# Tail of a hybrid decoder block: the norm's multiply moves from GpSimd to VectorE, token tile 0's scaling to ScalarE, and the last pieces change order

## Chip, cores and metric

One core of a Trainium2 chip runs the kernel. The time is device microseconds of one execution, median of several. Engines: PE (TensorE) multiplies matrices, VectorE (DVE) and ScalarE (ACT) work element by element, GpSimd (POOL) likewise, SyncE (SP) issues the transfers.

## What is computed

A block of 256 tokens and width 2048 in float32. The last stage, which the change touches, takes the merged branches, multiplies by one more matrix, adds the residual with a gate and normalises each token's row:

```python
merged = jax.nn.sigmoid(g_a) * y_a + jax.nn.sigmoid(g_b) * y_b
x = x + gate[:, None, :] * (merged @ w_out[l])
...
def rms_norm(x, w):
    xf = x.astype(jnp.float32)
    y = xf * lax.rsqrt(jnp.mean(xf * xf, axis=-1, keepdims=True) + EPS)
    return (y * w.astype(jnp.float32)).astype(x.dtype)
...
return rms_norm(x, normf_w)
```

So each output row needs the sum of squares over all of its 2048 columns before any of it can be scaled and stored.

## The kernel before

The kernel streams its weights as units of 128 x 1024 in the order of a list, `UNITS`. Each float32 weight is split by ScalarE and VectorE into a high and a low part (L288, L294), and PE multiplies three times (high by high, low by high, high by low; L322 and L334). Instructions are issued to each engine's queue in the order in which the Python code writes them; an engine takes its queue in that order, and waits are inserted where one instruction overwrites or reads what another engine reads or writes.

The output projection is the last stage: 32 units, k = 0 to 15 by two halves of 1024 columns. There are two token tiles, t = 0 and 1, of 128 tokens each. For each token tile and half there is one PSUM tile of two banks (`cur[t, half]`, 2 x 512 columns). In units with k under 12 both token tiles are multiplied as the weights come; the weights of the last four k (`KEEP`) are kept in SBUF (keepH, keepL), and there token tile 0 is finished first (L888) and evicted in four chunks of 512 columns (L892).

Then comes the tail (L898 to L916): token tile 1's last four k, piece by piece in the order of `TAIL` (L45). A piece (lo, n) covers n columns from lo; lo under 1024 is half 0, lo from 1024 on half 1, and within a half 512 columns make a bank. So 0 is half 0, first bank; 512 and 768 are half 0, second bank; 1024 and 1280 are half 1, first bank; 1536 and 1792 are half 1, second bank. Each piece is 4 x 3 matmuls (L906), followed by its eviction, `out_evac`:

- L765, VectorE: r = PSUM times the gate;
- L766, VectorE: r = r + residual;
- L772, ScalarE: Square of r, summed over the columns into one number per token (a second instruction, the accumulator read, belongs to it); the squares themselves overwrite the residual, which is done with;
- L774, GpSimd: r = r times the norm's weights, in place. For tile 1's columns from 1536 on this is left to L804.

After the first piece `out_root(0)` adds up tile 0's sums (L791, VectorE) and takes the root (L792, ScalarE). Two calls of `out_finish(0, ...)`, after the third and the fourth piece, scale tile 0: a reciprocal (L799, VectorE), then for even chunks L806 on VectorE, for odd ones L808 on ScalarE, each with its store (L809, SyncE). `out_partial` (L783 to L786, VectorE) sums tile 1's numbers as far as they are there, `out_root(1)` (L794, ScalarE) and `out_finish(1, ...)` end the kernel with a reciprocal, four scalings and four stores.

Of the kernel before, what the change touches and what calls it, by code (L numbers as in the profile page):

```python
# [19 lines left out]
AF = mybir.ActivationFunctionType  # L20
ALU = mybir.AluOpType
PSUM = bass.MemoryType.PSUM

S, D, NH, DK, DV = 256, 2048, 8, 128, 256
# [17 lines left out]
KEEP = 4  # L42
WARM = (9, 16)

TAIL = ((0, 512), (1024, 512), (512, 256), (1536, 256), (768, 256), (1792, 256))  # L45


def units():
# [26 lines left out]
def alt(x):  # L75

    return x.rearrange("p (a n) -> p n a", a=2)
# [13 lines left out]
def body(ctx: ExitStack, tc: tile.TileContext, wu, wa, xT_d, x_d, cols_d, rows_d, out_d):  # L91
    nc = tc.nc
    act, dve, pool, pe, sync = nc.scalar, nc.vector, nc.gpsimd, nc.tensor, nc.sync
# [9 lines left out]
    def slot(tag, shape, name, dt=F32):  # L103
        return slots.tile(shape, dt, name=name, tag=tag)
# [83 lines left out]
    for i in range(2):  # L188
        cp = psum("g", f"c{i}")
        cps.append(cp)  # L190
        for b in range(2):
            lo = 1024 * i + 512 * b
# [132 lines left out]
    def stationary(a, k, t):  # L325

        return a[:, k, 128 * t:128 * t + 128] if a is hH or a is hL else a[:, k, t:S:2]
# [13 lines left out]
    def run_fillers(n):  # L341
        for _ in range(min(n, len(fillers) + len(later))):
            (fillers or later).popleft()()
# [388 lines left out]
    fin = {}  # L732
# [23 lines left out]
    def out_evac(t, lo, n, p):  # L756

        if "r" not in fin:
            fin["r"] = slot("s7", [128, 2, D], "r")
            fin["ss"] = slot("fss", [128, 2, 4], "fss")  # L760
            fin["ssl"] = slot("fssl", [128, 4], "fssl")
            fin["tot"] = slot("tot", [128, 2, 1], "tot")
        cs = slice(lo, lo + n)
        r, x = fin["r"][:, t, cs], ml["x"][:, t, cs]
        dve.tensor_tensor(r, p, fin["gate_b"][:, cs], op=ALU.mult)  # L765
        dve.tensor_tensor(r, r, x, op=ALU.add)  # L766
        if n == 512:
            ss = fin["ss"][:, t, lo // 512:lo // 512 + 1]
        else:
            i = TAIL.index((lo, n)) - len(TAIL) + 4  # L770
            ss = fin["ssl"][:, i:i + 1]
        act.activation(x, r, AF.Square, accum_out=ss)  # L772
        if not t or lo < 1536:
            pool.tensor_tensor(r, r, norm_row(lo, n), op=ALU.mult)  # L774

    def norm_row(lo, n):
        return fin["nf", lo // 1024][:, lo % 1024:lo % 1024 + n]

    def out_partial(step):

        ss, sl = fin["ss"][:, 1, :], fin["ssl"]
        if step == 0:
            dve.tensor_scalar(ss[:, 1:2], ss[:, 0:1], ss[:, 2:3], sl[:, 0:1], op0=ALU.add, op1=ALU.add)  # L783
        else:
            dve.tensor_scalar(ss[:, 1:2], ss[:, 1:2], sl[:, 1:2], sl[:, 2:3], op0=ALU.add, op1=ALU.add)
            dve.tensor_scalar(ss[:, 3:4], ss[:, 1:2], 1.0 / D, EPS, op0=ALU.mult, op1=ALU.add)  # L786

    def out_root(t):
        tot = fin["tot"][:, t, :]
        if t == 0:  # L790
            dve.tensor_reduce(tot, fin["ss"][:, t, :], axis=mybir.AxisListType.X, op=ALU.add)  # L791
            act.activation(tot, tot, AF.Sqrt, bias=eps_c, scale=1.0 / D)  # L792
        else:
            act.activation(tot, fin["ssl"][:, 3:4], AF.Sqrt, bias=fin["ss"][:, t, 3:4], scale=1.0 / D)  # L794

    def out_finish(t, chunks):
        tot = fin["tot"][:, t, :]
        if 0 in chunks:
            dve.reciprocal(tot, tot)  # L799
        for c in chunks:  # L800
            cs = slice(512 * c, 512 * c + 512)
            r = fin["r"][:, t, cs]
            if t and c == 3:
                dve.scalar_tensor_tensor(r, r, tot, norm_row(512 * c, 512), op0=ALU.mult, op1=ALU.mult)  # L804
            elif c % 2 == 0:
                dve.tensor_scalar(r, r, tot, None, op0=ALU.mult)  # L806
            else:
                act.activation(r, r, AF.Copy, scale=tot)  # L808
            sync.dma_start(out_d[128 * t:128 * t + 128, cs], r)  # L809
# [7 lines left out]
    for n, (kind, grp, k, half) in enumerate(UNITS):  # L817
# [28 lines left out]
        elif kind == "if":  # L846
# [4 lines left out]
            for b in range(8):  # L851
                kk = 8 * k + b
                c = slice(128 * b, 128 * b + 128)
# [28 lines left out]
        else:  # L882
# [6 lines left out]
            if kept:  # L889
                if k == 15:  # L890
                    for b in range(2):
                        out_evac(0, 1024 * half + 512 * b, 512, cur[0, half][:, b, :])  # L892
            else:
                mm_token(cur[1, half], w, 0, hb["mH"], hb["mL"], k, 1, k == 0, False)
                head.pop(n)
                rest.pop(n)
            run_fillers(len(fillers) if kept else 1)
    for lo, n in TAIL:  # L898
        half, c0 = divmod(lo, 1024)
        b, at_b = divmod(c0, 512)  # L900
        p = cur[1, half][:, b, at_b:at_b + n]
        for k in range(16 - KEEP, 16):
            u = NU - 2 * (16 - k) + half
            for a, w in ((hb["mH"], head[u]), (hb["mH"], rest[u]), (hb["mL"], head[u])):
                wb = alt(w[:, 512 * b:512 * b + 512])[:, at_b // 2:(at_b + n) // 2, :]
                pe.matmul(p, lhsT=stationary(a, k, 1), rhs=wb, start=False,  # L906
                          stop=k == 15 and w is head[u] and a is hb["mL"], skip_group_check=True)
        out_evac(1, lo, n, p)
        if (lo, n) == TAIL[0]:
            out_root(0)  # L910
        elif (lo, n) in TAIL[2:4]:
            out_finish(0, (0, 1) if (lo, n) == TAIL[2] else (2, 3))
        if (lo, n) in (TAIL[3], TAIL[5]):
            out_partial(TAIL.index((lo, n)) - 3)
    out_root(1)
    out_finish(1, (0, 2, 1, 3))  # L916


# [59 lines left out]
```

## Time and profile before

| | us |
|---|---|
| median of 3 runs | 1179.76 (1177.83 to 1180.12) |
| the profiled execution | 1177.47 |
| its span, first to last instruction | 1175.8 |
| PE busy | 1152.4 (98%) |
| VectorE busy | 809.7 (69%) |
| ScalarE busy | 572.7 (49%) |
| GpSimd busy | 16.6 (1%) |
| first eviction begins (L765) | 1152.81 |
| last matmul begins | 1166.97 |

The shares are means over stages with different limits; for a change in the tail only the last 24 us count. In rows of the timeline the first number is the start in us from the start of the span, the second the duration; a row with xN merges N instructions that follow each other; brackets give how long the engine was idle before the row and which instruction's end released it. A busy PE is not PE at its peak. PEclk is the clock granted to PE as a share of 2.4 GHz.

### The profile page before, as it was taken

To read this page: it belongs to the slowest core of one execution; us is meant where nothing else is said; L and a number is where in the kernel's file an instruction comes from. 1 tells how busy PE (TensorE), PEld (TensorE's weight loads), DVE (VectorE), ACT (ScalarE), POOL (GpSimd) and SP (SyncE) were. 2 spreads that over 40 slices of the span, in tenths; PEclk is the share of its full clock that TensorE was granted. 3 is DMA by queue.
4 is the path that set the end of the run, shared out by engine and by line. 5 is a ranking of instruction groups with operands and counts; after the bars stand their busy time and mean duration, and the time that the engine had idled before them with its cause. 6 is when DMAs were issued, how large, how long until landed. Compare 5 with 4: busy or idle time off the path is not lost.

```text
span 1175.8 us, 21120 instructions
## 1 busy us (share of the span) xinstructions
PE 1152.4 (98%) x8738; PEld 1103.6 (94%) x8738; DVE 809.7 (69%) x1000; ACT 572.7 (49%) x670; POOL 16.6 (1%) x26
## 2 busy tenths in 40 slices
PE   8999999999999999999999999999999999999996
PEld 7898889988888999999999999999999999999995
DVE  6889998876888966655587465565564555556466
ACT  6754344464353556444556643533533443444452
POOL 0000000000000000000000000000000000000003
PEclk9999999999999999999999999999999999999999
DMA  9999899888788855544457556566556555486652
GB/s 342 389 382 361 324 367 357 310 324 298 256 319 306 317 198 182 196 151 156 162 178 268 196 184 214 182 198 210 188 197 205 197 196 191 144 289 219 219 204 72
DMA packets 79905, 283.57 MB, mean 241 GB/s; under 512 B 10689, under 2 KB 10817, under 8 KB 79425
## 3 DMA queue, kind: packets, MB, share of 16 engines
q1 hardware_dynamic: 79810, 282.23, 67.6%
q8 instruction: 68, 1.11, 0.4%
q14 instruction: 27, 0.22, 0.1%
HBM read 280.09 MB, written 2.11 MB: 240 GB/s over the span
## 4 chain that ended last, share of the span: by engine, by line
PE 80%; DVE 4%; issue 1%; DMA 1%; ACT 0%; DVEq 0%; SPq 0%; ACTq 0%
PE gB L322 7%; PE u L322 7%; PE yB L322 7%; PE yA L322 7%; PE C L322 7%; PE zb L322 7%; PE B L322 7%; PE qk L322 7%; PE out L334 6%; PE z L334 5%; PE gA L322 5%; PE o L334 2%; DVE wl L294 1%; PE v L334 1%; PE num L573 1%
## 5 line engine op out<-in xcount | busy, mean ns | idle before, releaser
L294 DVE TENSOR_TENSOR wl<-raw,wh 128x1024 fp32r<-128x1024 f32 x408 | 495.7, 1222 | 301.5 <-ACT wh L288 299.2
L288 ACT ACTIVATE wh<-raw 128x1024 fp32r<-128x1024 f32 x409 | 431.4, 1059 | 471.3 <-PE yB L322 47.0
L247 DVE SCALAR_TENSOR_TENSOR ada<-ada,c_b 128x1024 f32<-128x1024 f32 x96 | 116.9, 1218 | 1.2 <-DMA ada<-wa 1.2
L322 PE MATMUL gB<-hH,wh 128*128 128x256 f32 x256 | 40.0, 279 | 0.7 <-ACT wh L288 0.7
L334 PE MATMUL o<-wh,hH 128*128 128x512 f32 x128 | 38.2, 380 | 2.0 <-DVE v_ext L383 1.6
L334 PE MATMUL v<-wh,hH 128*128 128x512 f32 x128 | 38.2, 380 | 1.5 <-DVE o L383 1.5
L322 PE MATMUL gB<-hH,wl 128*128 128x256 f32 x256 | 39.2, 276 | 0.1
L322 PE MATMUL B<-hH,wh 128*128 128x256 f32 x256 | 39.3, 276 | 0.0
L334 PE MATMUL v<-wl,hH 128*128 128x512 f32 x128 | 38.2, 380 | 1.1 <-DVE wl L294 1.1
L322 PE MATMUL u<-hH,wh 128*128 128x256 f32 x256 | 39.1, 275 | 0.0
L322 PE MATMUL C<-hH,wh 128*128 128x256 f32 x256 | 39.1, 275 | 0.0
L322 PE MATMUL gB<-hL,wh 128*128 128x256 f32 x256 | 39.0, 275 | 0.0
L322 PE MATMUL u<-hL,wh 128*128 128x256 f32 x256 | 39.0, 275 | 0.0
L322 PE MATMUL u<-hH,wl 128*128 128x256 f32 x256 | 39.0, 275 | 0.0
L322 PE MATMUL C<-hL,wh 128*128 128x256 f32 x256 | 39.0, 275 | 0.0
L322 PE MATMUL C<-hH,wl 128*128 128x256 f32 x256 | 39.0, 275 | 0.0
L322 PE MATMUL B<-hL,wh 128*128 128x256 f32 x256 | 39.0, 275 | 0.0
L322 PE MATMUL B<-hH,wl 128*128 128x256 f32 x256 | 39.0, 275 | 0.0
L322 PE MATMUL zb<-hH,wh 128*128 128x256 f32 x256 | 39.0, 275 | 0.0
L322 PE MATMUL zb<-hL,wh 128*128 128x256 f32 x256 | 39.0, 275 | 0.0
L322 PE MATMUL zb<-hH,wl 128*128 128x256 f32 x256 | 39.0, 275 | 0.0
L322 PE MATMUL yA<-haH,wh 128*128 128x256 f32 x256 | 39.0, 275 | 0.0
(243 smaller groups left out, 2460.9 us busy)
## 6 DMA issues: line engine op xcount, KB each, us to landing
raw<-wu SPq DMA_DIRECT2D x418, 512.0 KB, 4.2
ada<-wa SPq DMA_DIRECT2D x96, 512.0 KB, 5.9
xT<-xT SPq DMA_DIRECT2D x4, 512.0 KB, 6.8
x_res<-x SPq DMA_DIRECT2D x1, 2048.0 KB, 10.0
out<-r SPq DMA_DIRECT2D x8, 256.0 KB, 2.8
z<-rows SPq DMA_DIRECT2D x2, 512.0 KB, 7.1
hn<-rows SPq DMA_DIRECT2D x2, 512.0 KB, 8.1
o<-rows SPq DMA_DIRECT2D x2, 512.0 KB, 6.9
```

What stands on the lines that cost most here:

```text
L247: dve.scalar_tensor_tensor(t, t, 1.0, c_b[:, half * 1024:half * 1024 + 1024], op0=ALU.mult, op1=ALU.mult, accum_out=acc[:, part, k, half:h ...
L288: act.activation(head[n], r, AF.Copy)
L294: dve.tensor_tensor(rest[n], r, head[n].bitcast(F32), op=ALU.subtract)
L322: pe.matmul(o, lhsT=w[:, j + 128 * b:j + 128 * b + 128], rhs=alt(block(h)), start=st and b % 2 == 0, stop=en and b % 2 == 1, skip_group_ch ...
L334: pe.matmul(o[:, b, :], lhsT=stationary(a, k, t), rhs=alt(ww[:, c0 + 512 * b:c0 + 512 * b + 512]), start=st, stop=en, skip_group_check=True)
L573: pe.matmul(p[:, t, :VW], lhsT=d, rhs=v, start=(i == 0), stop=(i == len(terms) - 1))
```

## The change

All edits are in the tail. In `out_evac` the multiply by the norm's weights (L774) goes from GpSimd's queue to VectorE's, at the same place of the code. In `out_finish` VectorE keeps only chunk 0 (by L806) and chunk 3 (by L804) of tile 1; all four chunks of tile 0 and chunks 1 and 2 of tile 1 go to ScalarE, tile 0's four are done in one call after the second piece, and tile 1's order is 3, 1, 0, 2 instead of 0, 2, 1, 3. `TAIL` has seven pieces instead of six: 512 columns, then 256 each, in the order half 0 second bank, half 1 first bank, half 1 second bank, and once more. The sums of squares are kept in six places instead of four and added in three steps, after the fourth, sixth and seventh piece.

```diff
--- before.py
+++ after.py
@@ -42,7 +42,7 @@
 KEEP = 4
 WARM = (9, 16)
 
-TAIL = ((0, 512), (1024, 512), (512, 256), (1536, 256), (768, 256), (1792, 256))
+TAIL = ((0, 512), (512, 256), (1024, 256), (1536, 256), (768, 256), (1280, 256), (1792, 256))
 
 
 def units():
@@ -758,7 +758,7 @@
         if "r" not in fin:
             fin["r"] = slot("s7", [128, 2, D], "r")
             fin["ss"] = slot("fss", [128, 2, 4], "fss")
-            fin["ssl"] = slot("fssl", [128, 4], "fssl")
+            fin["ssl"] = slot("fssl", [128, 6], "fssl")
             fin["tot"] = slot("tot", [128, 2, 1], "tot")
         cs = slice(lo, lo + n)
         r, x = fin["r"][:, t, cs], ml["x"][:, t, cs]
@@ -767,11 +767,11 @@
         if n == 512:
             ss = fin["ss"][:, t, lo // 512:lo // 512 + 1]
         else:
-            i = TAIL.index((lo, n)) - len(TAIL) + 4
+            i = TAIL.index((lo, n)) - 1
             ss = fin["ssl"][:, i:i + 1]
         act.activation(x, r, AF.Square, accum_out=ss)
         if not t or lo < 1536:
-            pool.tensor_tensor(r, r, norm_row(lo, n), op=ALU.mult)
+            dve.tensor_tensor(r, r, norm_row(lo, n), op=ALU.mult)
 
     def norm_row(lo, n):
         return fin["nf", lo // 1024][:, lo % 1024:lo % 1024 + n]
@@ -780,9 +780,11 @@
 
         ss, sl = fin["ss"][:, 1, :], fin["ssl"]
         if step == 0:
-            dve.tensor_scalar(ss[:, 1:2], ss[:, 0:1], ss[:, 2:3], sl[:, 0:1], op0=ALU.add, op1=ALU.add)
+            dve.tensor_scalar(ss[:, 1:2], ss[:, 0:1], sl[:, 0:1], sl[:, 1:2], op0=ALU.add, op1=ALU.add)
+        elif step == 1:
+            dve.tensor_scalar(ss[:, 1:2], ss[:, 1:2], sl[:, 2:3], sl[:, 3:4], op0=ALU.add, op1=ALU.add)
         else:
-            dve.tensor_scalar(ss[:, 1:2], ss[:, 1:2], sl[:, 1:2], sl[:, 2:3], op0=ALU.add, op1=ALU.add)
+            dve.tensor_scalar(ss[:, 1:2], ss[:, 1:2], sl[:, 4:5], None, op0=ALU.add)
             dve.tensor_scalar(ss[:, 3:4], ss[:, 1:2], 1.0 / D, EPS, op0=ALU.mult, op1=ALU.add)
 
     def out_root(t):
@@ -791,7 +793,7 @@
             dve.tensor_reduce(tot, fin["ss"][:, t, :], axis=mybir.AxisListType.X, op=ALU.add)
             act.activation(tot, tot, AF.Sqrt, bias=eps_c, scale=1.0 / D)
         else:
-            act.activation(tot, fin["ssl"][:, 3:4], AF.Sqrt, bias=fin["ss"][:, t, 3:4], scale=1.0 / D)
+            act.activation(tot, fin["ssl"][:, 5:6], AF.Sqrt, bias=fin["ss"][:, t, 3:4], scale=1.0 / D)
 
     def out_finish(t, chunks):
         tot = fin["tot"][:, t, :]
@@ -802,7 +804,7 @@
             r = fin["r"][:, t, cs]
             if t and c == 3:
                 dve.scalar_tensor_tensor(r, r, tot, norm_row(512 * c, 512), op0=ALU.mult, op1=ALU.mult)
-            elif c % 2 == 0:
+            elif t and c == 0:
                 dve.tensor_scalar(r, r, tot, None, op0=ALU.mult)
             else:
                 act.activation(r, r, AF.Copy, scale=tot)
@@ -906,14 +908,15 @@
                 pe.matmul(p, lhsT=stationary(a, k, 1), rhs=wb, start=False,
                           stop=k == 15 and w is head[u] and a is hb["mL"], skip_group_check=True)
         out_evac(1, lo, n, p)
-        if (lo, n) == TAIL[0]:
+        i = TAIL.index((lo, n))
+        if i == 0:
             out_root(0)
-        elif (lo, n) in TAIL[2:4]:
-            out_finish(0, (0, 1) if (lo, n) == TAIL[2] else (2, 3))
-        if (lo, n) in (TAIL[3], TAIL[5]):
-            out_partial(TAIL.index((lo, n)) - 3)
+        elif i == 1:
+            out_finish(0, (0, 1, 2, 3))
+        if i in (3, 5, 6):
+            out_partial({3: 0, 5: 1, 6: 2}[i])
     out_root(1)
-    out_finish(1, (0, 2, 1, 3))
+    out_finish(1, (3, 1, 0, 2))
 
 
 def kernel(**inputs):
```

## Rows read from the trace of the kernel before

**Rows 1.** Busy us by engine in one stretch; then PEclk, DMA share, GB/s.

```profile
1155.00:1160.00 5.00, 4.64 (x23) 3.92 (x22) 4.89 (x7) 2.17 (x6) 4.93 (x3) 1.00 0.00 0
```

**Rows 2.** Chain that ended last, from 1100 us: by line, then pieces in time.

```profile
by line: PE out L334 69.6%; DVE r L766 10.5%; DVE r L765 6.7%; DVE r L806 2.8%; DVE r L804 0.9%; ACT x_res L772 0.7%; issue 0.6%; DVEq L974 0.5%; ACT tot L794 0.4%; DVE tot L799 0.3%; DVE fss L783 0.2%; DVE tot L791 0.1%; DVEq L806 0.1%
...
1160.64 0.07 DVE tot L791
...
1166.44 0.18 DVE fss L783
...
1169.11 0.17 DVE tot L799
```

**Rows 3.** VectorE's timeline of the tail: start, us, line, out<-in.

```profile
1152.81 0.69 DVE L765 TENSOR_TENSOR r<-out,gate_b 128x512 f32<-128x512 f32 x1 [5.25 <-PE out L334]
1153.54 0.69 DVE L766 TENSOR_TENSOR r<-r,x_res 128x512 f32<-128x512 f32 x1
1154.15 0.68 DVE L765 TENSOR_TENSOR r<-out,gate_b 128x512 f32<-128x512 f32 x1
...
1156.19 1.07 DVE L766 TENSOR_TENSOR r<-r,x_res 128x512 f32<-128x512 f32 x1
...
1163.93 1.24 DVE L806 TENSOR_SCALAR r<-r,tot 128x512 f32<-128x512 f32 x1
...
1166.99 0.42 DVE L766 TENSOR_TENSOR r<-r,x_res 128x256 f32<-128x256 f32 x1
1167.33 0.42 DVE L765 TENSOR_TENSOR r<-out,gate_b 128x256 f32<-128x256 f32 x1
1167.78 0.43 DVE L766 TENSOR_TENSOR r<-r,x_res 128x256 f32<-128x256 f32 x1
...
1170.18 0.75 DVE L804 SCALAR_TENSOR_TENSOR r<-r,tot,nf 128x512 f32<-128x512 f32 x1
```

**Rows 4.** PE's timeline of the tail; in brackets idle before it and releaser.

```profile
1153.91 0.38 PE L906 MATMUL out<-keepH,mH 128*128 128x512 f32 x1
...
1158.87 0.38 PE L906 MATMUL out<-keepH,mL 128*128 128x512 f32 x1
1159.61 0.38 PE L906 MATMUL out<-keepH,mH 128*128 128x256 f32 x1 [0.36 <-DVE r L765]
...
1165.57 0.39 PE L906 MATMUL out<-keepH,mH 128*128 128x256 f32 x1 [1.09 <-DVE r L765]
...
1166.97 0.28 PE L906 MATMUL out<-keepH,mL 128*128 128x256 f32 x1
```

**Rows 5.** GpSimd's timeline of the tail.

```profile
1155.07 10.69 POOL L774 TENSOR_TENSOR r<-r,nf 128x512 f32<-128x512 f32 x7 [448.51 <-ACT x_res L772]
1168.03 0.76 POOL L774 TENSOR_TENSOR r<-r,nf 128x256 f32<-128x256 f32 x1 [2.27 <-ACT x_res L772]
```

**Rows 6.** Groups by line and shape, 1105 us on: xcount, busy us, mean ns.

```profile
L766 DVE TENSOR_TENSOR r<-r,x_res 128x512 f32<-128x512 f32 x6 | 5.6, 925 | 0.2
...
L766 DVE TENSOR_TENSOR r<-r,x_res 128x256 f32<-128x256 f32 x4 | 2.4, 602 | 0.1
```

**Rows 7.** ScalarE's timeline of the tail.

```profile
1154.26 0.64 ACT L772 ACTIVATE x_res<-r 128x512 f32<-128x512 f32 x1 [7.96 <-DVE r L766]
1154.80 0.19 ACT L772 ACTIVATION_READ_ACCUMULATOR x_res<-r 128x1 f32 x1
...
1167.45 0.42 ACT L772 ACTIVATE x_res<-r 128x256 f32<-128x256 f32 x1 [0.25 <-DVE r L766]
1167.77 0.19 ACT L772 ACTIVATION_READ_ACCUMULATOR x_res<-r 128x1 f32 x1
...
1169.37 0.72 ACT L808 ACTIVATE r<-r,tot 128x512 f32<-128x512 f32 x1 [0.29 <-DVE tot L799]
```

**Rows 8.** Busy us by engine in one stretch, with the granted clock (PEclk).

```profile
1171.00:1172.00 1.00, 0.00 (x0) 0.00 (x0) 0.00 (x0) 0.00 (x0) 0.00 (x0) 0.65 1.04 373
```

**Rows 9.** SyncE's issues of the last four stores, the first three merged.

```profile
1169.90 1.29 SPq L809 DMA_DIRECT2D out<-r  x3
```

## The prediction

> **What bounds the kernel now.** The page's busy shares (PE nearly throughout, GpSimd next to nothing) say little of a change to the last 24 us. The table of busy time by stretch does: from 1155 to 1160 us VectorE is busy 4.89 of 5.00 us, GpSimd 4.93, PE 4.64 [rows 1]. Then the chain that ended last: once PE's run of L334 is over, it is VectorE lines one after another (L766 10.5% of that window, L765 6.7%, L806 2.8%; ScalarE's two 1.1%) [rows 2]. So the tail is **VectorE's queue**, from the first eviction at 1152.81 us [rows 3] to the end of the last reciprocal, 1169.11 + 0.17 = 1169.28 [rows 2]: 16.47 us. PE waits for it, not the other way round: the third piece's first matmul sat 0.36 us and the sixth's 1.09 us until a VectorE L765 was done [rows 4]. What the change does to this queue it does to the kernel.
>
> Two things about the queue matter. VectorE is slowed while GpSimd multiplies (from 1155.07 on [rows 5]): the 512-column add L766 took 0.69 us at 1153.54 and 1.07 at 1156.19, a scaling L806 took 1.24 at 1163.93 [rows 3], and the means of L766, 0.925 and 0.602 us [rows 6], stand against 0.69 and 0.42 undisturbed [rows 3]. And each multiply by the norm's weights overwrites r, which ScalarE's Square still reads: GpSimd began its first one at 1155.07, 0.08 us after ScalarE's accumulator read ended (1154.80 + 0.19), and idled 2.27 us for that same line before its last one [rows 5, 7]. On GpSimd this wait holds nobody up.
>
> **The change part by part.** *The multiply moves to VectorE*, behind L766 in program order and in front of the next L765, and its wait for Square comes with it. Queued behind the waiting multiply are the next piece's L765 and L766; for that L765 wait PE's later pieces, and for that L766 ScalarE's next Square. For 512 columns: L765 to L766 0.73 (1152.81 to 1153.54), L766 0.69, hand-over 0.03 (1154.23 to 1154.26), Square with its accumulator read 0.73 (1154.26 to 1154.99), hand-over back taken as 0.03 too (GpSimd's 0.08 is its upper end), and the multiply, priced as L766, the other operation with two SBUF inputs: 0.61 from its start to the next start (1153.54 to 1154.15) [rows 3, 5, 7]. Sum **2.82 us a piece**, five pieces (four of token tile 0, one of tile 1): 14.10. For 256 columns: 0.45 (1167.33 to 1167.78), 0.42, 0.04, 0.51 (1167.45 to 1167.96), 0.03, 0.34 (1166.99 to 1167.33) [rows 3, 7]: **1.79 us**, four pieces (512, 768, 1024, 1280): 7.16. Ends: if Square itself and not its accumulator read lets the multiply go, 0.09 less on each, 0.8 in all; with GpSimd's hand-over 0.05 more on each, 0.45; with L804's 0.75 [rows 3] for the 512-column multiply 0.06 more on five, 0.3. GpSimd's slowing is gone: all these durations are undisturbed ones.
>
> *Seven pieces for six.* 1536 and 1792 get no multiply; 1536 costs 0.45 + 0.34 = 0.79. Two partial sums ahead of the last piece at 0.18 each (L783): 0.36. Tile 0's reduce 0.07, its reciprocal 0.17 [rows 2]. The last piece: L765 to L766 0.45, and from there to the end of the reciprocal 1.50 as now, also with two small sums in it (1167.78 [rows 3] to 1169.28).
>
> *ScalarE scales all four chunks of tile 0*, in one go after the second piece. A scaling starts 0.09 after the reciprocal's end (1169.28 to 1169.37) and takes 0.72 [rows 2, 7]; a ScalarE instruction starts about 0.1 before the end of the one in front (the accumulator read at 1154.80, Square's end at 1154.90 [rows 7]), so four take 4 x 0.62 = 2.48, and ScalarE is free 2.57 us after the reciprocal. VectorE has the third piece's L765 and L766 done 0.87 after it; its Square could begin at 0.90 and begins at 2.57: the third piece's multiply waits **1.67 us** more. The two L806 of tile 0 leave VectorE; they are not in the sum. The four stores of tile 0 are issued from one place of SP's queue; only the last four stores stand behind them, over 8 us later, so they cost nothing.
>
> *Three banks in turn.* Before, the third piece (half 0, second bank) waited for the first piece's eviction (half 0, first bank): it starts at 1159.61, with 0.36 us of idling put down to L765 [rows 4], though nothing had been read from its own bank. So the wait goes by the tile of two banks. Then the new second piece (half 0 again) waits for the first one's L765, which starts at 1152.81 + 4 x 2.82 = 1164.09 and ends 0.69 later, at 1164.78. PE, done with the first piece near 1156.5 (24 matmuls from 1153.91 to about 1159.1, half of them [rows 4]), idles 8.3 us. Now the clock: at the end of the kernel PE stops at 1166.97 + 0.28 = 1167.25 [rows 4], and the granted clock averages 0.65 in the microsecond from 1171 [rows 8]; between the levels 1.0 and 0.5 (2.4 and 1.2 GHz) this is a fall at 1171.3, 4.05 us after the stop. So 8.3 us should bring it down. A 256-column piece took 1165.57 to 1167.25 = 1.68 us at 2.4 GHz [rows 4]; my estimate at 1.2 GHz is twice that, 3.36. The second piece is then ready at 1164.82 + 3.36 + 0.04 = 1168.22, and VectorE asks for it at 1152.81 + 14.10 + 0.07 = 1166.98: **1.24 us** (none at 2.4 GHz: ready at 1166.54). The third piece, 2.9 behind, is hidden under ScalarE's four scalings. No row shows the clock rise, so this has two ends: back before the fourth piece is wanted (8 us after PE resumes), nothing more; down to the end, some 6 us more (rivals). I take the first, since PE works through most of those 8 us. The Trainium skill (TensorE: Matmul & The Clock Gate, section "What's actually happening") has the throttled clock as the default and activity as what releases it; by it the first end holds; no row here shows it. The seventh piece waits for the sixth's L765 (same tile): ready 0.41 + 0.05 + 1.68 + 0.04 = 2.18 after that one starts, where VectorE is there after 1.79 + 0.18 = 1.97: **0.21**.
>
> **Sum:** 14.10 + 0.07 + 1.24 + 7.16 + 0.17 + 1.67 + 0.79 + 0.36 + 0.21 + 0.45 + 1.50 = 27.72 us, against 16.47: +11.25. The last stores: SP issues them about 0.45 apart, the first when its chunk is done (three from 1169.90 to 1171.19 [rows 9]). That chunk was a half-microsecond scaling; in the new order it is L804's 0.75 [rows 3], some 0.11 behind the reciprocal, so done at 0.86 instead of 1169.90 - 1169.28 = 0.62: +0.25. In all **+11.5 us**. The profiled execution took 1177.47 (span 1175.8, 1.67 around it), which gives 1189.0; it lies 2.29 under the median of the three runs, and the comparison is with the median: 1179.76 + 11.5 = **1191.3**.
>
> **The rivals.**
> *The clock stays down to the end.* The third piece comes 2.9 behind the second, its L765 runs to 1171.5; the fourth is ready 3.4 later, at 1174.9 (VectorE: 1173.6), the fifth at 1177.8, the sixth at 1180.7, the seventh 3.45 after the sixth's L765, at 1184.6; with 0.45 + 1.50 that is 1186.5, 17.2 over 1169.28, and with the 0.25 +17.5: 1197.3. For it: PE works in bursts. Against: second and third piece alone are over 6 us of work at that level.
> *The clock does not fall.* Against: 8.3 us is twice the 4.05. 1.24 goes: 1190.0.
> *The banks are free of each other*, so four pieces run on at once and PE waits for its own bank only. Against: the third piece's wait [rows 4]. All pieces then lie ready before VectorE asks, at either clock; 1.24 and 0.21 go: +10.0, 1189.8. The Trainium skill (PSUM — Partial Sum Buffer, section "PSUM bank collisions raise a hardware error") asks for a guard by bank, no wider; by it this case would hold; the rows differ from it.
> *Not slower: Square does not hold the multiply.* Place: nine multiplies. A 512 piece would take 0.73 + 0.61 + 0.61 = 1.95, a 256 piece 0.45 + 0.34 + 0.34 = 1.13, and the scalings would hold nobody: 0.87 x 5 + 0.66 x 4 + 1.67 = 8.7 us go, and with the banks free too the sum is +1.3: 1181.1. It decides if these waits together stay under 1 us. For it: ScalarE has room. Against: GpSimd shows the wait, on the same operand. Even this is no gain: the multiplies add 5 x 0.61 + 4 x 0.34 = 4.4 us to a queue without gaps; GpSimd's slowing of L766 (6 x 0.235 + 4 x 0.182 = 2.1 [rows 6]) and two L806 (1.24 and under 0.75) give back less.
>
> **How the numbers follow.** About 0.2%, 2.4 us, is what a measurement of this kernel can tell from no change. Chances: forecast 0.63, clock down to the end 0.14, clock not fallen 0.07, banks free 0.09, multiply not held 0.07. The time is the likeliest one's. The first four lie from 1189.8 to 1197.3; the runs of before reach 1.9 under their median, so the range is 1187.8 to 1197.3, which also takes in the ends of the unknown prices. Slower by over 0.2%: 0.63 + 0.14 + 0.07 + 0.09 = 0.93; within: 0.06; faster, an unheld multiply with a low run: 0.01.
>
> **What the profile after would show.** VectorE idle before nearly every L774, released by ScalarE's L772, some 0.75 us for 512 and 0.55 for 256 columns; starts of the first five L765 2.8 us apart, the first piece's near 1164.1; PE idle 8 us after the first piece, released by L765; granted clock 0.5 in the second piece; one longer wait at the third piece, behind four L808; the last reciprocal ending near 1180.5. Wrong if L765 starts come under 2 us apart (multiply not held), if PE runs four pieces without a stop (banks), or if the clock stays 1.00 or never returns.

## The result and the profile after

| | before | after |
|---|---|---|
| median of 4 runs each, us | 1178.83 (1177.83 to 1180.12) | 1190.95 (1190.0 to 1194.09) |
| ratio | | 1.0103 [1.009, 1.0116] |
| span of the profiled execution | 1175.8 | 1192.3 |
| first eviction of the tail (L765) begins | 1152.81 | 1158.62 |
| tail: from there to the end of the last reciprocal | 16.46 | 27.19 |
| from there to the end of the span | 6.53 | 6.49 |

The kernel is 12.1 us slower (10.6 to 13.7 by the interval). The two profiled spans differ by more, 16.5 us. Of that 10.73 is the tail. The other 5.8 lies ahead of the tail's first eviction, which came between 1152.8 and 1158.6 us in the twelve profiled executions of this study, whatever was edited in the tail; the last section shows the two places where the execution of after lost it. So kernels are compared below by the tail's length, and by their medians beside it.

The tail of after on VectorE. Columns: start, us, engine, line, operation, then in brackets the idle time before it and what ended it. Lines left out repeat the first three (the first five pieces) or the pattern of 256 columns, or are small sums.

```profile
1158.62 0.69 DVE L765 TENSOR_TENSOR r<-out,gate_b 128x512 f32<-128x512 f32 x1 [5.22 <-PE out L334]
1159.35 0.69 DVE L766 TENSOR_TENSOR r<-r,x_res 128x512 f32<-128x512 f32 x1
1160.83 0.69 DVE L774 TENSOR_TENSOR r<-r,nf 128x512 f32<-128x512 f32 x1 [0.79 <-ACT x_res L772]
1161.44 0.68 DVE L765 TENSOR_TENSOR r<-out,gate_b 128x512 f32<-128x512 f32 x1
...
1169.86 0.68 DVE L765 TENSOR_TENSOR r<-out,gate_b 128x512 f32<-128x512 f32 x1
...
1172.67 0.15 DVE L793 TENSOR_REDUCE tot<-fss 128x1 f32<-128x4 f32 x1
1173.57 0.42 DVE L765 TENSOR_TENSOR r<-out,gate_b 128x256 f32<-128x256 f32 x1 [0.75 <-PE out L908]
...
1175.03 0.43 DVE L774 TENSOR_TENSOR r<-r,nf 128x256 f32<-128x256 f32 x1 [0.58 <-ACT x_res L772]
1175.37 0.16 DVE L801 RECIPROCAL tot<-tot 128x1 f32<-128x1 f32 x1
1175.74 0.42 DVE L765 TENSOR_TENSOR r<-out,gate_b 128x256 f32<-128x256 f32 x1 [0.21 <-PE out L908]
...
1178.56 0.43 DVE L774 TENSOR_TENSOR r<-r,nf 128x256 f32<-128x256 f32 x1 [1.94 <-ACT x_res L772]
1178.90 0.42 DVE L765 TENSOR_TENSOR r<-out,gate_b 128x256 f32<-128x256 f32 x1
...
1179.70 0.27 DVE L783 TENSOR_SCALAR fss<-fss,fssl 128x1 f32<-128x1 f32 x1
1179.88 0.41 DVE L765 TENSOR_TENSOR r<-out,gate_b 128x256 f32<-128x256 f32 x1
...
1183.46 0.27 DVE L785 TENSOR_SCALAR fss<-fss,fssl 128x1 f32<-128x1 f32 x1
1183.87 0.42 DVE L765 TENSOR_TENSOR r<-out,gate_b 128x256 f32<-128x256 f32 x1
...
1185.65 0.16 DVE L801 RECIPROCAL tot<-tot 128x1 f32<-128x1 f32 x1 [0.59 <-ACT tot L796]
```

Before [rows 3] one piece's L765 followed the last one's L766 without a gap. Now each piece of 512 columns has a hole of 0.79 us ahead of its multiply, put down to ScalarE's L772, and these pieces come 2.82 apart (1158.62 to 1161.44; the mean of the five is 2.81). The waits of the last 43 us, summed (engine, what it waits with, releaser: us in total, times, the longest):

```profile
PE out L908 <- DVE r L765: 9.7, 3, 8.1
DVE r L774 <- ACT x_res L772: 7.6, 9, 1.9
DVE r L765 <- PE out L908: 1.0, 2, 0.7
```

All nine multiplies wait for a Square, 7.6 us together. ScalarE's rows show when it lets go: the first multiply starts at 1160.83, 0.03 after the accumulator read's end (1160.61 + 0.19).

```profile
1160.07 0.63 ACT L772 ACTIVATE x_res<-r 128x512 f32<-128x512 f32 x1 [7.93 <-DVE r L766]
1160.61 0.19 ACT L772 ACTIVATION_READ_ACCUMULATOR x_res<-r 128x1 f32 x1
...
1175.56 2.56 ACT L810 ACTIVATE r<-r,tot 128x512 f32<-128x512 f32 x4 [0.57 <-DVE tot L801]
1178.03 0.40 ACT L772 ACTIVATE x_res<-r 128x256 f32<-128x256 f32 x1
```

The last two rows are tile 0's four scalings and, behind them, the third piece's Square: the one long wait, 1.94 us.

PE (start, us), and busy time by stretch (us; PE, PEld, DVE, ACT, POOL busy; PEclk, DMA share, GB/s):

```profile
1162.09 0.38 PE L908 MATMUL out<-keepH,mL 128*128 128x512 f32 x1
1170.60 0.58 PE L908 MATMUL out<-keepH,mH 128*128 128x256 f32 x1 [8.13 <-DVE r L765]
1170.97 0.42 PE L908 MATMUL out<-keepL,mH 128*128 128x256 f32 x1
...
1176.44 0.28 PE L908 MATMUL out<-keepL,mH 128*128 128x256 f32 x1
...
1182.14 0.39 PE L908 MATMUL out<-keepH,mH 128*128 128x256 f32 x1 [1.08 <-DVE r L765]
```

```profile
1164.00:1165.00 1.00, 0.00 (x0) 0.00 (x0) 0.96 (x3) 0.00 (x0) 0.00 (x0) 0.93 0.00 0
1165.00:1170.00 5.00, 0.00 (x0) 0.00 (x0) 3.39 (x6) 1.44 (x4) 0.00 (x0) 0.50 0.00 0
1170.00:1175.00 5.00, 4.40 (x20) 4.40 (x21) 2.85 (x6) 1.53 (x5) 0.00 (x0) 0.50 0.00 0
1175.00:1176.00 1.00, 0.70 (x6) 0.51 (x4) 0.76 (x3) 0.44 (x1) 0.00 (x0) 0.95 0.00 0
```

The second piece, in a bank that nobody reads, waits 8.13 us for the first piece's eviction, and runs at 1.2 GHz (granted clock 0.50). The clock is back just after 1175.0, when the last stretch begins. In the chain that ended last, L774 is new with 9.4% of the last 43 us, ScalarE's L772 has 11.4% and its scalings 7.6% (L810: tile 0's four, and one of tile 1 at the end); before, the chain ran through ScalarE for two short steps only [rows 2]:

```profile
by line: PE out L334 20.1%; DVE r L765 11.7%; ACT x_res L772 11.4%; PE out L908 10.8%; DVE r L766 10.6%; DVE r L774 9.4%; ACT r L810 7.6%; issue 1.8%; ACTq L977 1.4%; ACT tot L796 0.7%; DVE tot L801 0.6%; DVE fss L783 0.4%
```

### The profile page after: what moved, and what is told of

Same layout as the page of the kernel before. It is cut to its first block, busy times and chain, and to the rows that moved or that the text cites. A ratio compares the mean times of both kernels' runs of the same rounds, so it can differ in the third digit from the quotient of the medians.

```text
span 1192.3 us, 21145 instructions
## 1 busy us (share of the span) xinstructions
PE 1158.2 (97%) x8750; PEld 1108.6 (93%) x8750; DVE 811.5 (68%) x1009; ACT 575.0 (48%) x675; POOL 5.1 (0%) x18
## 4 chain that ended last, share of the span: by engine, by line
PE 80%; DVE 3%; ACT 1%; DMA 1%; issue 0%; ACTq 0%
PE gB L322 7%; PE u L322 7%; PE yB L322 7%; PE yA L322 7%; PE zb L322 7%; PE B L322 7%; PE C L322 7%; PE qk L322 7%; PE out L334 6%; PE z L334 5%; PE gA L322 5%; PE v L334 3%; PE o L334 2%; DVE wl L294 1%; PE num L573 1%; DMA raw<-wu 1%
## 5 line engine op out<-in xcount | busy, mean ns | idle before, releaser
L288 ACT ACTIVATE wh<-raw 128x1024 fp32r<-128x1024 f32 x409 | 431.6, 1060 | 474.5 <-PE yB L322 47.5
## 6 DMA issues: line engine op xcount, KB each, us to landing
x_res<-x SPq DMA_DIRECT2D x1, 2048.0 KB, 10.6
```

Source lines behind the costliest of these rows:

```text
L288: act.activation(head[n], r, AF.Copy)
```

## Experiments

There were two theories from the start. The first is the forecast's: the multiply is costly because it waits in VectorE's queue for ScalarE's Square, and order and scalings add some 3 us (1.24, 0.21 and 1.67 in its sum). The rival: it costs what VectorE computes, and the order of pieces makes the rest. All results stand in one table, with 4 to 12 runs of each kernel. Each ratio is taken against runs of before on the same chip as the kernel's own (their medians lie between 1178.83, which is the one in the table, and 1180.18), and its interval holds what the tail and the end part alone would give.

| kernel | median, us | ratio [95%] | tail, us |
|---|---|---|---|
| before | 1178.83 | 1 | 16.46 |
| after | 1190.95 | 1.0103 [1.009, 1.0116] | 27.19 |
| before, multiply on VectorE (1) | 1186.96 | 1.0054 [1.0036, 1.0072] | 24.40 |
| the same, without the hold (2) | 1181.67 | 1.0009 [0.9997, 1.0021] | 18.86 |
| the same, multiply one piece later (3) | 1180.89 | 1.0006 [0.9996, 1.0015] | 17.71 |
| after, without the hold (4) | 1186.8 | 1.0068 [1.0043, 1.0093] | 23.63 |
| after, multiply left on GpSimd (5) | 1183.85 | 1.0033 [1.0021, 1.0044] | 20.67 |
| after, pieces 2 and 3 exchanged (6) | 1188.62 | 1.0081 [1.0061, 1.0102] | 26.34 |
| after, PE kept busy (7) | 1188.09 | 1.0078 [1.0059, 1.0096] | 26.35 |
| after, scalings spread (8) | 1189.8 | 1.0087 [1.0064, 1.0111] | 26.38 |
| before, tile 0 scaled on ScalarE (9) | 1178.93 | 0.9991 [0.998, 1.0001] | 15.81 |
| before, one scaling moved (10) | 1179.09 | 0.9993 [0.9982, 1.0003] | 16.08 |

**1. Only the multiply moves.**

```diff
-            pool.tensor_tensor(r, r, norm_row(lo, n), op=ALU.mult)
+            dve.tensor_tensor(r, r, norm_row(lo, n), op=ALU.mult)
```

> The kernel before with one edit of the change: the multiply on VectorE instead of GpSimd, in place as in the change; order of the pieces and scalings as before. Theory (the hold by Square is most of the loss): tail 24.5 us, 8.0 over before's 16.5, every L774 on VectorE idling 0.5 to 0.8 us for L772. Rival (the order of the pieces and the scalings on ScalarE are the main part): tail under 20 us.

The tail is 24.40 us, +7.94, as expected, and three quarters of what the whole change adds to it (0.54% of 1.03% by the medians, with wide intervals). Its waits:

```profile
DVE r L774 <- ACT x_res L772: 5.9, 8, 0.8
```

Eight multiplies wait 5.9 us; the rest of the 7.94 is what VectorE now computes, less what GpSimd no longer slows.

**2. The same without what makes it wait.** The Square writes its squares to a tile of its own and the multiply writes where they used to go, so neither overwrites what the other reads. The scalings then read from there. A cut is marked by three dots.

```diff
-        act.activation(x, r, AF.Square, accum_out=ss)
...
+        act.activation(fin["junk"][:, 0:n], r, AF.Square, accum_out=ss)
-            pool.tensor_tensor(r, r, norm_row(lo, n), op=ALU.mult)
+            dve.tensor_tensor(x, r, norm_row(lo, n), op=ALU.mult)
...
-            r = fin["r"][:, t, cs]
+            r = fin["r"][:, t, cs] if t and c == 3 else ml["x"][:, t, cs]
```

> The kernel before with the multiply on VectorE, but not held: it writes into the residual's place and Square writes to a scratch tile; order of the pieces and scalings as before; nothing is left out. Theory (VectorE's queue has no gaps, so nine multiplies of 0.61 and 0.34 us add more than the end of GpSimd's slowing gives back): tail about 17.9 us, 1.4 over before and 6.6 under the held form of the same kernel. Rival (GpSimd's slowing of VectorE was the larger part): tail under 16.5, faster than before.

The waits are gone and 5.54 of the 7.94 us with them: this shows that the hold is the larger part. The size was missed: the tail is 18.86 where 17.9 was expected. One piece (the multiply is L776 here):

```profile
1155.74 0.69 DVE L765 TENSOR_TENSOR r<-out,gate_b 128x512 f32<-128x512 f32 x1 [5.06 <-PE out L334]
1156.47 0.69 DVE L766 TENSOR_TENSOR r<-r,x_res 128x512 f32<-128x512 f32 x1
1157.19 0.69 DVE L776 TENSOR_TENSOR x_res<-r,nf 128x512 f32<-128x512 f32 x1
1157.80 0.68 DVE L765 TENSOR_TENSOR r<-out,gate_b 128x512 f32<-128x512 f32 x1
```

An instruction that reads the result of the one just before it starts 0.72 to 0.73 after that one's start (L766 behind L765, L776 behind L766); one that doesn't starts 0.61 after (L765 behind L776). The multiply had been priced with the second distance and stands in the first: 2.06 a piece, not 1.95.

**3. The multiply one piece later.** Issued behind the next piece's L765 and L766, it finds Square over and does not follow what it reads.

```diff
+        if "due" in fin:
+            q, qlo, qn = fin.pop("due")
+            dve.tensor_tensor(q, q, norm_row(qlo, qn), op=ALU.mult)
...
-            pool.tensor_tensor(r, r, norm_row(lo, n), op=ALU.mult)
+            fin["due"] = r, lo, n
```

> The kernel before with the multiply by the norm's weights on VectorE in its place, issued behind the next piece's two instructions instead of directly behind its own piece's, so that ScalarE's square is over by then; order of pieces and scalings as before. Theory (the multiply cost 2.82 - 1.95 us a piece because it stood in VectorE's queue waiting for the square, and an instruction that needs the one just before it starts 0.12 us later than one that doesn't): no waits on the square, pieces of 512 columns 1.95 us apart, tail 17.9 to 18.0, time 1.5 us (0.13%) over before. Rival (0.72 a multiply wherever it stands): 2.06 apart, tail 18.9, 2.4 us over before. Third case (the hold is not the cause): 2.82 apart, tail over 24.

```profile
1159.14 0.69 DVE L766 TENSOR_TENSOR r<-r,x_res 128x512 f32<-128x512 f32 x1
1159.75 0.69 DVE L775 TENSOR_TENSOR r<-r,nf 128x512 f32<-128x512 f32 x1
1160.35 0.69 DVE L765 TENSOR_TENSOR r<-out,gate_b 128x512 f32<-128x512 f32 x1
```

The pieces come 1.93 apart, no multiply waits for ScalarE, and the tail is 17.71 (+1.25), 0.2 under what was expected. This is the price of the multiply on VectorE when its place in the queue is right: 6 x 0.60 + 2 x 0.34 = 4.3 us of work, of which 3.0 comes back, since L766 and L806 are no longer slowed by GpSimd (0.69 and 0.48 us each here for 512 columns; before, the L766 took up to 1.07 and the first L806 1.24). Same instruction, same engine: +7.94 at one place of the queue, +1.25 at another. The rival theory falls for the multiply: what VectorE computes is the small part. It still doesn't beat before.

**4. All of after without the hold.** The edit of 2, made to after.

> The changed kernel, but the multiply writes into the residual's place and Square writes its squares into a scratch tile, so that VectorE's multiply need not wait for ScalarE; nothing is left out. Tail means first eviction's start to the end of the last reciprocal: 16.5 us before, 27.2 us after. Theory (the hold by Square is most of the loss): VectorE's idle time in front of L774 (7.6 us over nine multiplies) disappears, L765 starts of token tile 0 come 1.95 us apart instead of 2.81, and PE, which now waits for evictions tile by tile, sets part of what is left: tail 21 to 23 us, 4 to 6.5 us faster than after, still 4 to 6 us slower than before. Rival (VectorE simply has more to do, the hold costs little): L765 starts stay about 2.8 apart and the tail stays over 26 us.

It missed: 23.63, not 21 to 23. The waits on Square are gone, but VectorE now waits 4.4 us for PE, in five places (the three longest are shown):

```profile
1167.88 0.43 DVE L765 TENSOR_TENSOR r<-out,gate_b 128x256 f32<-128x256 f32 x1 [1.50 <-PE out L910]
...
1170.30 0.42 DVE L765 TENSOR_TENSOR r<-out,gate_b 128x256 f32<-128x256 f32 x1 [1.00 <-PE out L910]
...
1172.51 0.43 DVE L765 TENSOR_TENSOR r<-out,gate_b 128x256 f32<-128x256 f32 x1 [0.87 <-PE out L910]
```

PE itself waited 5.12 us for the first piece's eviction, and the granted clock was 0.50 from 1164 to 1170; how much of the 4.4 us is the clock and how much the wait was not tried. So two waits lie on top of each other in after: while VectorE stands before a Square, PE makes the piece that VectorE would else wait for.

**5. All of after, the multiply left on GpSimd.** What the new order and the scalings cost by themselves.

> The changed kernel with the multiply left on GpSimd: only the order of the pieces and the scalings on ScalarE are changed. Theory (a wait of GpSimd holds nobody up, but a piece waits for its PSUM tile's last eviction): the second piece starts about 0.7 us late, the others lose some at the fourth and seventh piece; tail 18.5 to 19.5 us, 2 to 3 over before, and no waits of VectorE for L772. Rival (three banks in turn help PE): tail at or under 16.5.

It missed upwards as well: 20.67, +4.21, with VectorE waiting for PE 5.25 us (1.88, 0.76, 1.33, 0.44, 0.84). The second piece's first matmul shows why:

```profile
1161.93 0.58 PE L908 MATMUL out<-keepH,mH 128*128 128x256 f32 x1 [2.92 <-DVE r L765]
1162.31 0.42 PE L908 MATMUL out<-keepL,mH 128*128 128x256 f32 x1
```

PE idled 2.92 us, and the piece ran at the low clock all the same (granted 0.98 from 1161 to 1162, 0.50 from 1162 to 1165). The tail of before had shown the fall 4.05 us after a stop [rows 8]. In the old order the second piece lies in the other half and needs no eviction, so PE has 512 columns to work on while VectorE is in tile 0. The order (with the scalings) and the multiply together cost 10.73, singly 4.21 and 7.94: 1.4 us of the one hide in the other, as in 4.

**6. Pieces 2 and 3 exchanged**, so that the second piece is in the other half.

```diff
-TAIL = ((0, 512), (512, 256), (1024, 256), (1536, 256), (768, 256), (1280, 256), (1792, 256))
+TAIL = ((0, 512), (1024, 256), (512, 256), (1536, 256), (768, 256), (1280, 256), (1792, 256))
```

> The changed kernel with the second and third piece exchanged, so that the second piece lies in the other PSUM tile than the first. Theory (a piece waits for the last eviction of its tile of two banks): the second piece runs on right behind the first, the third waits 7 us for the first piece's L765; VectorE's 0.75 us of waiting at the second piece's L765 goes, and the tail is 26.5 us instead of 27.2. Rival (waits go by the bank): neither order waits there, the tail is the same within 0.2 us.

**7. PE kept busy** between piece 1 and 2 with 30 matmuls into a PSUM tile that nobody reads.

```diff
+            idle_bank = psum("g", "idle_bank")
+            for _ in range(30):
+                pe.matmul(idle_bank[:, 0, 0:128], lhsT=ones, rhs=ones, start=True, stop=True)
```

> The changed kernel with 30 matmuls more on a free PSUM tile between the first and the second piece, whose results nobody reads; they fill some 7 us of PE's 8.1 us of waiting. Theory (part of the loss is PE's clock at 1.2 GHz after the wait): the granted clock stays 1.00, the second piece's matmuls come 0.12 us apart instead of 0.21, VectorE's 0.75 us of waiting at the second piece and 0.21 at the third go, of which the 0.21 was hidden by ScalarE's four scalings; tail 26.4 to 26.6 us, 0.7 faster. Rival (the wait for the eviction itself and not the clock is what costs): tail stays at 27.2. Either way the clock is a small part of the 10.7 us.

Both take away the second piece's late arrival by different means, and both save the same, a little more than expected: 0.85 and 0.84 us. With the exchange, the second piece follows the first without a stop and the wait moves to the third:

```profile
1156.57 0.27 PE L908 MATMUL out<-keepH,mH 128*128 128x256 f32 x1
...
1164.86 0.58 PE L908 MATMUL out<-keepH,mH 128*128 128x256 f32 x1 [6.71 <-DVE r L765]
...
1168.87 0.41 DVE L765 TENSOR_TENSOR r<-out,gate_b 128x256 f32<-128x256 f32 x1
```

The third piece runs at the low clock there (granted 0.50 from 1161 to 1170), but it is done near 1167.8, before VectorE asks for it at 1168.87: made early enough, this piece costs nothing at the low clock.

With the added matmuls the wait for L765 stays (1.44 us after the last of them), but the piece runs at 2.4 GHz and is there in time:

```profile
1164.98 0.39 PE L908 MATMUL out<-keepH,mH 128*128 128x256 f32 x1 [1.44 <-DVE r L765]
1165.20 0.28 PE L908 MATMUL out<-keepL,mH 128*128 128x256 f32 x1
```

So the clock costs the tail of after 0.8 us. And the wait behind it goes by the tile of two banks: in kernel 6 the second piece, in the other tile, does not wait, and the third does, though nobody reads its own bank.

**8. Tile 0's four scalings spread**, one behind each of the pieces 2 to 5.

```diff
-        elif i == 1:
-            out_finish(0, (0, 1, 2, 3))
+        elif i < 5:
+            out_finish(0, (i - 1,))
```

> The changed kernel with token tile 0's four scalings on ScalarE placed one behind each of the second to fifth piece instead of all four behind the second. Theory (four scalings in one go hold the third piece's Square and so VectorE's multiply): the third multiply's wait falls from 1.94 to about 0.58 us like the others, no other multiply's wait grows, and the tail is 0.9 to 1.4 us shorter, less than the whole 1.36 where PE's fourth piece is then the late one. Rival (the scalings only fill time in which VectorE waits anyway): the wait moves to a later piece and the tail stays within 0.3 us of 27.2.

The third multiply waits 0.58 like the others, 1.36 less, and the tail gains 0.81, less than the 0.9 to 1.4 expected: 0.32 and 0.35 us of waiting for PE come up at the fourth and fifth piece, which the long wait had hidden.

```profile
1174.56 0.42 DVE L774 TENSOR_TENSOR r<-r,nf 128x256 f32<-128x256 f32 x1 [0.58 <-ACT x_res L772]
1175.30 0.42 DVE L765 TENSOR_TENSOR r<-out,gate_b 128x256 f32<-128x256 f32 x1 [0.32 <-PE out L908]
```

**9 and 10. Only the scalings move**, in the old order with the multiply on GpSimd: both of VectorE's scalings of tile 0, then one of them.

```diff
-            elif c % 2 == 0:
+            elif t and c % 2 == 0:
```

> The kernel before with one edit: all four chunks of token tile 0 are scaled on ScalarE; GpSimd keeps the multiply and the pieces their order. Theory (VectorE's queue is the bound, and two L806 of 1.2 and 0.4 us leave it): tail 15.0 to 15.6 us, about 1.2 us under before, that is 0.1%. Rival (ScalarE's scalings hold up Square and thereby the sums): tail within 0.3 us of 16.5.

```diff
-            elif c % 2 == 0:
+            elif c % 2 == 0 and (t or c):
```

> The kernel before with one of the scalings of the first token tile moved to ScalarE: of the two that VectorE makes there, one goes, one stays; the multiply stays on GpSimd and the order is the old one. Theory (the scalings on ScalarE cost the tail only where the last of them pushes the squares behind it past the sums): with one scaling fewer behind the squares than with all four on ScalarE, the 0.63 us wait of the sums goes and VectorE keeps one scaling more; tail about 15.4 us against 16.46 before, about 1 us (0.09%) under the time before. Rival (what VectorE keeps costs it as much as the wait): tail 15.6 to 15.9, as with all four, no difference to be seen in the time.

Both missed (15.81 where 15.0 to 15.6 was expected, 16.08 where 15.4 was), and no difference can be seen in either time. With both moved the tail is 0.65 shorter; the last sums then wait for a Square behind the scalings:

```profile
1171.71 0.27 DVE L785 TENSOR_SCALAR fss<-fss,fssl 128x1 f32<-128x1 f32 x1 [0.63 <-ACT x_res L772]
```

With one moved that wait is gone, as expected, and yet the gain is only 0.38: what VectorE then does is slowed by GpSimd in the place of what left, L766 to 1.00 and the scaling to 0.96 (before, the same two took 0.50 and 0.48, behind the scaling of 1.24).

```profile
1166.28 1.00 DVE L766 TENSOR_TENSOR r<-r,x_res 128x256 f32<-128x256 f32 x1
1167.20 0.96 DVE L806 TENSOR_SCALAR r<-r,tot 128x512 f32<-128x512 f32 x1
```

No kernel here beats before by more than a measurement can tell.

## Why the prediction was right

Forecast 1191.3 us, measured 1190.95; as a difference +11.5 forecast, +12.1 measured, of which the tail and the end part show 10.7. By steps, in us, the forecast beside the profiled tail:

| step | forecast | after |
|---|---|---|
| five pieces of 512 columns | 14.10 | 14.05 |
| reduce, second piece late | 1.31 | 0.90 |
| pieces 2, 3, 5, 6, tile 0's reciprocal, the scalings' wait | 9.00 | 8.91 |
| piece 1536 | 0.79 | 0.80 |
| two partial sums, seventh piece late | 0.57 | 0.59 |
| last piece to the end of the reciprocal | 1.95 | 1.94 |
| tail | 27.72 | 27.19 |

- *The hold.* 2.82 a piece forecast, 2.80 to 2.82 measured, with the accumulator read as what lets go and a hand-over of 0.03: the two choices made between ends were the right ones. 1.79 for 256 columns, 1.79 measured. Kernels 1 and 2 show that the hold is the cause.
- *The scalings.* Forecast 1.67 of extra wait at the third multiply; it was 1.36 (1.94 against 0.58), since that piece itself came 0.21 late behind PE, which the forecast had put entirely under the scalings. Both together are 1.57 of the 1.67; most of the rest is that the scalings began 0.03 after the reciprocal's end, not 0.09.
- *The second piece.* PE's 8.3 us of idling was 8.13, the granted clock fell to 0.50, and the wait was for the tile of two banks (kernel 6). The size was off: the reduce and the lateness took 0.90, not 1.31. The term that was mis-sized is the piece at 1.2 GHz, taken as twice 1.68: it took 2.94 (1170.60 to 1173.54). None of its parts doubled: from the first matmul to the second 0.22 became 0.37, the distance of the others 0.118 became 0.214, the last one's length 0.28 became 0.42.
- *The clock comes back.* Of the two ends the first held: 0.50 up to 1175, 0.95 in the microsecond after it, 4.5 us after PE resumed. The Trainium skill (TensorE: Matmul & The Clock Gate, section "What's actually happening") has activity release the throttled clock, and here the trace agrees.
- *The last stores.* +0.25 forecast. The first of the last four was issued 0.82 after the reciprocal's end (1186.63 against 1185.81), before 0.63: 0.19 later. The end part is no longer, though, 6.49 against 6.53; over the twelve kernels it lies between 6.20 and 6.57, so a term of this size can't be seen in it.
- *Rivals.* "The banks are free" fell: the 8.13 us wait is for another bank's reader. The Trainium skill (PSUM — Partial Sum Buffer, section "PSUM bank collisions raise a hardware error") asks for a guard by bank, or finer by bank and quadrant. This kernel's waits go by the whole tile, and no run here tried a tile of one bank. "The clock does not fall" fell with the 0.50, "down to the end" with its return. "Not held" fell as well, and kernel 4 shows that its size was too small besides: without the hold the tail is 23.63, +7.2, where that rival, with the banks free too, had +1.3. An unheld multiply takes 0.72 to 0.73 of the piece and not 0.61, and the 4.4 us that VectorE then waits for PE were not in its sum.

The forecast's closeness, 0.35 us, is better than its parts and in so far luck: the tail was forecast 0.5 too long and the end part 0.3, the medians stand 1.4 further apart than tail and end part account for, and before's median came out 0.9 lower with a run more. The 1.4 lies within the interval of the ratio; no cause of it was found in the tail, and it stays open.

## What to carry to other kernels

When an elementwise step moves from an idle engine to the one that sets the end, look at what it waits for before what it computes: here the same multiply cost 7.9 us in place and 1.25 us one piece later, because an engine that takes its queue in order passes its wait on to all that is queued behind. Pieces that follow each other should lie in different PSUM tiles as the program allocates them, since this program's waits go by the tile (0.85 us here, kernel 6). And two waits that overlap don't add: with one taken away, the other comes up (4, 5 and 8), so each must be tried alone and with the rest.

## What was not expected of the hardware

The granted clock did not fall at one fixed time after PE's stop. The end of the kernel before had shown 4.05 us [rows 8]. In the kernels here it was 2.3 us (kernel 6), 2.4 (after: stop at 1162.47, 0.93 from 1164 to 1165), 3.0 (kernel 5, just as PE took up work again), 3.4 (kernel 4) and 5.0 (kernel 8, whose stop of 8.13 us is the same as after's). In kernel 2 it fell 1.0 us after PE had resumed from a stop of 2.52. It came back 3.5 us (kernel 5: 0.81 from 1165 to 1166), 4.5 (after) and 5.8 (kernels 1 and 6) after PE resumed. So the forecast's 4.05 was one value out of several; the forecast of a fall held because PE's stop was longer than all of them. What makes the difference between these is not settled by these runs.

VectorE's distance from one start to the next depends on whether the second reads the first's result: 0.72 to 0.73 against 0.60 to 0.61 us for 512 columns, 0.45 to 0.46 against 0.34 for 256. Kernels 2 and 3 show it with the same two instructions: the multiply starts 0.72 after the L766 whose result it reads, and 0.61 after one whose result it doesn't read.

Ahead of the tail, executions differ by some us in places that no edit touched. In the execution of after the first 20 us had a stretch at the low clock, and from 368 us on a weight load stands in the chain for 7.11 us, where before the chain has other work. The splits of the weights on ScalarE (L288) date the loss: the first comes at 24.80 us, 2.84 later than in the execution of before, the one at 373.73 is 2.83 later, the next 5.81, and so it stays up to the tail, which begins 5.81 later. Kernel 9, in the old order, shows the same low clock at the start (0.65 from 10 to 15 us), so it does not come with the change. Of the twelve executions three had no such stretch (before, 6 and 7), and they reached the tail at 1152.8 to 1153.0 us, the nine others at 1154.9 or later. Busy time by stretch in after, then a piece of its chain:

```profile
10.00:15.00 5.00, 3.09 (x7) 2.50 (x8) 3.70 (x6) 4.97 (x6) 0.00 (x0) 0.61 1.03 416
```

```profile
368.30 7.11 DMA raw<-wu
```
